# The second norm in groups of tiles, its scale row read from PSUM

## The chip, the cores and the metric

The kernel runs on one core of a Trainium2 chip. The metric is the device time of one execution in microseconds (us). A core has five engines with queues of their own, which run side by side and wait for one another through semaphores: TensorE (PE: matmuls), VectorE (DVE), ScalarE (ACT), GpSimd (POOL) and SyncE (SP, which here issues the plain DMAs). SBUF is the working memory with 128 partitions; PSUM holds the results of the matmuls and has 8 banks of 512 float32 numbers per partition. POOL works in SBUF here, never in PSUM.

## The reference

One decoder layer over 2048 tokens of 1024 channels: four mixers (RWKV-7, gated linear attention, mLSTM, latent attention), a projection, a first norm, and then a mixture of 32 experts of which each token takes two. The change is in what follows the experts:

```python
x = layer_norm(DN_ALPHA * x + mix, ln1_g[i], ln1_b[i], LN_EPS)
ffn = hier_moe(x, moe_w_rg[i], ...)
ple = jax.nn.sigmoid(x @ ple_w_gate[i] + ple_b_gate[i]) * (p[i] @ ple_w[i])
x = layer_norm(DN_ALPHA * x + ffn + ple, ln2_g[i], ln2_b[i], LN_EPS)
```

The last line is the second norm. For each token it takes the mean and the variance over 1024 channels, subtracts the mean, multiplies by the inverse root of the variance and by a scale row `g`, and adds a bias row `b`; the same two rows serve all tokens.

## The kernel before

The tokens are cut into 16 tiles of 128, with one token per partition and 1024 channels in the free dimension. Tiles lie in pairs 0 to 7. The experts add their results to `accd` in DRAM by indirect DMAs from POOL. When the last of these has landed, `finish` (L2202) reads `accd` pair by pair, normalizes and writes `out`. For the last four tiles (12 to 15, "late") the term `ple` is not yet in `accd`; `finish` and the end of the expert loop compute it: `late_gate` (48 matmuls into one of two PSUM tiles `self.gu` of two banks each, then two DVE additions of the gate's bias at L2187 and a tanh on ACT), `late_embed` (12 matmuls into the PSUM tile `yb`, then one DVE operation, L2200, that reads `yb`), and an addition to the tile on POOL (L2237).

`norm2(out, p)` treats one pair:

- a load of the pair into a raw tile (L2233); there are five of these, so pairs 5 and 7 wait for the outputs of pairs 0 and 1. Pair 4 goes into a tile of another pool, `m_dl`;
- the statistics of each tile: two `bn_stats` and one `bn_aggr` on DVE (L2253, L2254), or, for tiles 1, 3, 5, 7, 9 and 11 (`ACT_STATS`), four ACT passes (L2243) with three small DVE instructions among them (L2247 to L2249);
- the inverse root for both tiles at once, on DVE: L2256, then `rsqrt` (L68, L69 and three rounds of L71, L72, L73), then L2258. All of these handle two numbers per partition. Eight pairs make eight roots;
- the end of each tile. For most tiles ACT applies mean and root (L2265), DVE multiplies by `g` (L2266) and POOL adds `b` (L2267). For tiles 3, 7, 11, 14 and 15 (`DVE_ENDS`) DVE does all of it in two passes: L2262 with `g`, L2263 with `b`;
- the output of the tile by SP (L2268).

`g` and `b` lie in SBUF, in the tiles `m_xg` that held the gathered rows of the experts. The pairs come in the order 0, 1, 2, 3, 6, 4, 5, 7, with the late gates and embeddings written between them. Each queue runs in order, but the order isn't that of the text: a planner sorts the ready instructions of each queue by its own estimate of their times when the kernel is built, so that steps of a root lie between passes of other tiles.

Of the kernel before, what the change touches and what calls it, by code (L numbers as in the profile page):

```python
# [8 lines left out]
F32 = mybir.dt.float32  # L9
# [4 lines left out]
AF = mybir.ActivationFunctionType  # L14
OP = mybir.AluOpType
# [5 lines left out]
D = 1024  # L21
# [9 lines left out]
class Layer:  # L31
# [28 lines left out]
        nc.tensor.matmul(out, lh, rl, start=False, stop=False)  # L60
        nc.tensor.matmul(out, ll, rh, start=False, stop=stop)  # L61

    def rsqrt(self, v, y, n, tag):
        nc = self.nc
        t = self.sm.tile([128, n], F32, name="rs_t" + tag)
        ti = t.bitcast(I32)
        p = v.shape[0]
        nc.vector.tensor_scalar(ti[:p], v.bitcast(I32), 1, None, op0=OP.logical_shift_right)  # L68
        nc.vector.tensor_scalar(y.bitcast(I32), ti[:p], -1.0, float(0x5F3759DF), op0=OP.mult, op1=OP.add)  # L69
        for _ in range(3):  # L70
            nc.vector.tensor_mul(t[:p], y, y)  # L71
            nc.vector.scalar_tensor_tensor(t[:p], t[:p], -0.5, v, op0=OP.mult, op1=OP.mult)  # L72
            nc.vector.scalar_tensor_tensor(y, t[:p], 1.5, y, op0=OP.add, op1=OP.mult)  # L73
# [2101 lines left out]
    def late_gate(self, t):  # L2175
        nc = self.nc
        xh, xl, _ = self.lx.pop(t)
        banks = [self.gu[t % 2][:, j] for j in range(2)]
        for k in range(8):
            w = self.lg[k]  # L2180
            for i, (a, b) in enumerate(((xh, 0), (xh, 1), (xl, 0))):
                for j, p in enumerate(banks):
                    nc.tensor.matmul(p, a[:, k], w[:, b, j * 512:j * 512 + 512], start=k == 0 and i == 0, stop=k == 7 and i == 2)
        gt = self.mw.tile([128, D], F32, name="m_y", bufs=3)
        for j, p in enumerate(banks):
            g = slice(j * 512, j * 512 + 512)
            nc.vector.tensor_add(gt[:, g], p, self.ln2[2][:, g])  # L2187
        nc.scalar.activation(gt, gt, AF.Tanh, scale=0.5)
        self.lt[t] = gt
# [12 lines left out]
    def finish(self, out):  # L2202
        nc = self.nc
        t = T - self.LATE
        self.late_p(t)
        self.late_p(t + 1)
        self.late_x(t + 2)
        self.norm2(out, 0)
        self.late_turn(t + 2)
        self.late_gate(t + 1)  # L2210
        self.late_embed(t)
        self.late_p(t + 2)
        self.norm2(out, 1)
        self.late_turn(t + 3)
        self.norm2(out, 2)
        self.late_gate(t + 2)
        self.late_embed(t + 1)
        self.late_p(t + 3)
        self.late_gate(t + 3)
        self.norm2(out, 3)  # L2220
        self.late_embed(t + 2)
        self.late_embed(t + 3)
        self.norm2(out, t // 2)
        self.norm2(out, 4)
        self.norm2(out, 5)
        self.norm2(out, t // 2 + 1)

    def norm2(self, out, p):
        nc, G = self.nc, 2
        g, b, _ = self.ln2  # L2230
        mv = self.sm.tile([128, G, 2], F32, name="f_mv")
        z = self.raw_tile() if p != 4 else self.wdn.tile([128, 2, D], F32, name="m_dl")
        nc.sync.dma_start(out=z, in_=self.pairs(self.accd, p))  # L2233
        for i in range(G):
            t = p * G + i
            if t in self.lt:
                nc.gpsimd.tensor_add(z[:, i], z[:, i], self.lt.pop(t))  # L2237
            if t in self.ACT_STATS:
                a = self.sm.tile([128, 4], F32, name="f_a")
                for f in range(2):  # L2240
                    for j in range(2):
                        junk = self.mw.tile([128, 512], F32, name="m_t", bufs=3)
                        nc.scalar.activation(junk, z[:, i, j * 512:j * 512 + 512], (AF.Identity, AF.Square)[f], accum_out=a[:, 2 * f + j:2 * f + j + 1],  # L2243
                                             **({"bias": m} if f else {}))
                    if f == 0:
                        m = self.sm.tile([128, 1], F32, name="f_m")
                        nc.vector.tensor_scalar(m, a[:, 0:1], a[:, 1:2], -1.0 / D, op0=OP.add, op1=OP.mult)  # L2247
                nc.vector.tensor_scalar(mv[:, i, 0:1], m, -1.0, None, op0=OP.mult)
                nc.vector.tensor_scalar(mv[:, i, 1:2], a[:, 2:3], a[:, 3:4], 1.0 / D, op0=OP.add, op1=OP.mult)  # L2249
                continue  # L2250
            st = self.sm.tile([128, 2, 6], F32, name="ln_st")
            for j in range(2):
                nc.vector.bn_stats(st[:, j], z[:, i, j * 512:j * 512 + 512])  # L2253
            nc.vector.bn_aggr(mv[:, i], st.rearrange("p a b -> p (a b)"))  # L2254
        v, rs, sh = (self.sm.tile([128, G], F32, name="f_" + n) for n in ("v", "rs", "sh"))
        nc.vector.tensor_scalar(v, mv[:, :, 1], 1e-5, None, op0=OP.add)  # L2256
        self.rsqrt(v, rs, G, "f")
        nc.vector.scalar_tensor_tensor(sh, mv[:, :, 0], -1.0, rs, op0=OP.mult, op1=OP.mult)  # L2258
        for i in range(G):
            t, zi = p * G + i, z[:, i]  # L2260
            if t in self.DVE_ENDS:
                nc.vector.scalar_tensor_tensor(zi, zi, mv[:, i, 0:1], g, op0=OP.subtract, op1=OP.mult)  # L2262
                nc.vector.scalar_tensor_tensor(zi, zi, rs[:, i:i + 1], b, op0=OP.mult, op1=OP.add)  # L2263
            else:
                nc.scalar.activation(zi, zi, AF.Identity, scale=rs[:, i:i + 1], bias=sh[:, i:i + 1])  # L2265
                nc.vector.tensor_mul(zi, zi, g)  # L2266
                nc.gpsimd.tensor_add(zi, zi, b)  # L2267
            nc.sync.dma_start(out=out[t * 128:t * 128 + 128], in_=zi)  # L2268


def layer(ctx, tc, I, out):
# [115 lines left out]
```

## Time and profile before

| what | us |
|---|---|
| median of 3 runs | 3073.34 (3070.55 to 3081.36) |
| time of the profiled execution | 3073.2 |
| its span in the trace | 3071.4 |
| DVE busy | 1962.6 (64%) |
| ACT busy | 1224.2 (40%) |
| POOL busy | 888.6 (29%) |

The page gives the busy time of each engine and cuts the span into 40 slices. The timeline has one row for each instruction (or a run of equal ones, with their count): its start in us from the start of the span, its duration, engine, line, operation, and the tensors written and read; in brackets stands how long the engine had been idle and what it waited for. [...]

### The profile page before, as it was taken

The numbers are of one execution on the slowest core, as the hardware profiler recorded it, in microseconds if no ns is written. First come the engines' busy times: TensorE is split into PE (matmuls) and PEld (weight loads), VectorE is DVE, ScalarE is ACT, GpSimd is POOL, SyncE is SP. The second block draws the span as 40 slices with busy tenths as digits, with TensorE's granted clock in tenths as the row PEclk, the third lists the DMA queues.
The fourth block names the chain that finished last, engine by engine and source line by source line (L and its number), as shares of the span: only waits on it lengthen the run. The fifth ranks groups of instructions, "written<-read, shape, count | busy, mean of one in ns | idle before, by whom it ended". The sixth has DMA issues, their size and how long they took to land. (4 is left out here: it accounts for less than half of the span.)

```text
span 3071.4 us, 42829 instructions
## 1 busy us (share of the span) xinstructions
PE 2818.2 (92%) x15420; PEld 2219.4 (72%) x15421; DVE 1962.6 (64%) x4100; ACT 1224.2 (40%) x2001; POOL 888.6 (29%) x552
## 2 busy tenths in 40 slices
PE   8999999998989999999999999899889988999883
PEld 6898877777867766666477799777667767777662
DVE  6366364456555567766656645576687756687869
ACT  4222132222124433333310222165576756666852
POOL 1000000001010023424521201445464544645624
PEclk9999999989989898989999999999999989999996
DMA  6332242122225522200243412377587867877863
GB/s 189 102 99 71 68 127 69 54 73 58 52 57 162 173 58 78 62 26 18 95 146 131 138 62 69 136 251 258 174 294 259 264 213 223 284 244 261 303 229 137
DMA packets 287042, 442.98 MB, mean 144 GB/s; under 512 B 84088, under 2 KB 152040, under 8 KB 286760
## 3 DMA queue, kind: packets, MB, share of 16 engines
q1 hardware_dynamic: 272200, 397.78, 39.0%
q0 software_dynamic: 14560, 41.47, 5.5%
q8 instruction: 172, 2.82, 0.4%
q14 instruction: 110, 0.90, 0.1%
HBM read 350.52 MB, written 96.50 MB: 146 GB/s over the span
## 5 line engine op out<-in xcount | busy, mean ns | idle before, releaser
L1884 PE MATMUL m_g<-m_g,xhl 128*128 128x512 f32 x2032 | 520.9, 405 | 20.1 <-PEq L2011 10.1
L1884 PEld LDWEIGHTS m_g<-m_g,xhl 128*128 128x128 f32 x2032 | 376.2, 192 | 113.6 <-issue 33.7
L1836 DVE TENSOR_TENSOR m_g<-m_raw,m_g 128x1024 fp32r<-128x1024 f32 x188 | 267.0, 1448 | 90.9 <-ACT m_g L1835 88.7
L1835 ACT CAST m_g<-m_raw 128x1024 fp32r<-128x1024 f32 x252 | 255.3, 1057 | 96.5 <-PEq L2011 80.3
L1916 PE MATMUL m_y<-m_dh,m_h 128*128 128x512 f32 x656 | 226.0, 410 | 26.4 <-ACT m_y L1923 8.0
L59 PE MATMUL pbank<-xh,wh 128*128 128x512 f32 x544 | 226.8, 417 | 7.0 <-DVE us L213 3.6
L60 PE MATMUL pbank<-xl,wh 128*128 128x512 f32 x544 | 219.3, 403 | 0.0
L61 PE MATMUL pbank<-xh,wl 128*128 128x512 f32 x544 | 218.8, 403 | 0.0
L51 ACT CAST xhl<-bank 128x512 fp32r<-128x512 f32 x204 | 117.3, 607 | 245.2 <-PE bank L1408 243.9
L1836 POOL TENSOR_TENSOR m_g<-m_raw,m_g 128x1024 fp32r<-128x1024 f32 x64 | 185.0, 2966 | 91.1 <-ACT m_g L1835 53.6
L1466 PE MATMUL wide<-wt,xhl 128*128 128x512 f32 x768 | 182.8, 397 | 3.6 <-ACT xhl L51 3.6
L1836 POOL TENSOR_TENSOR m_dl<-m_raw,m_dh 128x1024 fp32r<-128x1024 f32 x64 | 179.4, 2845 | 14.8 <-ACT m_dh L1835 14.6
L1304 POOL TENSOR_TENSOR mla_acc<-mla_acc,mla_pt 128x512 f32<-128x512 f32 (+3 forms) x112 | 132.4, 1182 | 148.5 <-ACT mla_pt L1302 132.0
L1466 PEld LDWEIGHTS wide<-wt,xhl 128*128 128x128 f32 x768 | 143.6, 189 | 39.6 <-ACT xhl L51 7.4
L1916 PEld LDWEIGHTS m_y<-m_dh,m_h 128*128 128x128 f32 x656 | 129.1, 197 | 58.9 <-ACT m_y L1923 10.7
L1302 ACT ACTIVATE mla_pt<-sbank 128x512 f32<-128x512 f32 (+3 forms) x160 | 85.2, 533 | 213.0 <-PE sbank L1298 104.0
L52 DVE TENSOR_TENSOR xhl<-bank,xhl 128x512 fp32r<-128x512 f32 x204 | 136.4, 684 | 48.8 <-ACT xhl L51 46.7
L1930 POOL DMA_INDIRECT accd<-m_y,m_put x47 | 95.7, 2037 | 245.0 <-ACT m_y L1923 125.5
L1646 PE MATMUL gate<-wt,xhl 128*128 128x354 f32 (+1 forms) x864 | 149.6, 330 | 1.4 <-ACT xhl L51 1.0
L59 PE MATMUL pbank<-wh,xh 128*128 128x256 f32 x512 | 150.7, 294 | 0.0
L60 PE MATMUL pbank<-wl,xh 128*128 128x256 f32 x512 | 149.1, 291 | 0.0
L1916 PE MATMUL m_y<-m_dl,m_h 128*128 128x512 f32 x360 | 146.5, 407 | 2.2 <-POOL m_dl L1836 2.2
(642 smaller groups left out, 6309.8 us busy)
## 6 DMA issues: line engine op xcount, KB each, us to landing
m_raw<-in_moe_w_down SPq DMA_DIRECT2D x64, 1024.0 KB
m_raw<-in_moe_w_gate SPq DMA_DIRECT2D x126, 512.0 KB
m_raw<-in_moe_w_up SPq DMA_DIRECT2D x126, 512.0 KB
wraw<-in_w_in SPq DMA_DIRECT2D x80, 256.0 KB
o_x<-in_x SPq DMA_DIRECT2D x16, 512.0 KB
x1d<-m_g SPq DMA_DIRECT2D x16, 512.0 KB
accd<-wide SPq DMA_DIRECT2D x16, 512.0 KB
m_raw<-accd SPq DMA_DIRECT2D x7, 1024.0 KB
```

What stands on the lines that cost most here:

```text
L51: nc.scalar.copy(hi, src)
L52: (eng and nc.gpsimd or nc.vector).tensor_sub(lo, src, hi.bitcast(F32))
L59: nc.tensor.matmul(out, lh, rh, start=start, stop=False)
L60: nc.tensor.matmul(out, lh, rl, start=False, stop=False)
L61: nc.tensor.matmul(out, ll, rh, start=False, stop=stop)
L1304: (nc.vector if kt in self.SUMS else nc.gpsimd).tensor_add(acc[:, c0 * 128:512], acc[:, c0 * 128:512], pt[:, 0:n])
L1466: nc.tensor.matmul(p[:, j], a[:, k], W[k][bb][:, j * 512:j * 512 + 512], start=k == 0 and i == 0, stop=k == 7 and i == 2)
L1646: nc.tensor.matmul(p[:, 0:n], a[:, k], b[:, o:o + n], start=k == 0 and i == 0, stop=k == 7 and i == 2)
L1835: self.nc.scalar.copy(h[:, i], raw[:, i])
L1836: lo_eng.tensor_sub(l[:, i], raw[:, i], h[:, i].bitcast(F32))
L1884: self.mark["pe"] = self.nc.tensor.matmul(banks[:, j], a, b[:, k % 2, j * 512:j * 512 + 512], start=k == 0 and i == 0, stop=k == 7 and i = ...
L1916: self.nc.tensor.matmul(p[:, j], a, b[:, k % 2, j * 512:j * 512 + 512], start=k == 0 and i == 0, stop=k == 3 and i == len(ps) - 1)
```

## The change

The norm goes in groups of pairs: (0), (1, 2), (3, 4), (6, 5), (7). All tiles of a group share one root, so there are five roots, with two or four numbers per partition. The order of pairs becomes 0, 1, 2, 3, 4, 6, 5, 7. Of the two PSUM tiles in `self.gu`, the late gates now all use the first one; the second, which the experts are done with, receives a copy of the scale row `g` by two ACT copies at the start of `finish`, and L2262 and L2266 read `g` from there. The small tiles of the norm move to another pool. The diff, cut to its core:

```diff
@@ rsqrt
-        t = self.sm.tile([128, n], F32, name="rs_t" + tag)
+        t = pool.tile([128, 4], F32, name="rs_t" + tag)[:, 0:n] if pool else self.sm.tile([128, n], F32, name="rs_t" + tag)
@@ late_gate
-        banks = [self.gu[t % 2][:, j] for j in range(2)]
+        banks = [self.gu[0][:, j] for j in range(2)]
@@ finish
         self.late_x(t + 2)
+        self.gain = self.gu[1].rearrange("p j d -> p (j d)")
+        for j in range(2):
+            self.nc.scalar.copy(self.gu[1][:, j], self.ln2[0][:, j * 512:j * 512 + 512])
         self.norm2(out, 0)
         self.late_turn(t + 2)
         self.late_gate(t + 1)
         self.late_embed(t)
         self.late_p(t + 2)
-        self.norm2(out, 1)
         self.late_turn(t + 3)
-        self.norm2(out, 2)
+        self.norm2(out, 1, 2)
         self.late_gate(t + 2)
         self.late_embed(t + 1)
         self.late_p(t + 3)
         self.late_gate(t + 3)
-        self.norm2(out, 3)
+        self.norm2(out, 3, 4)
         self.late_embed(t + 2)
         self.late_embed(t + 3)
-        self.norm2(out, t // 2)
-        self.norm2(out, 4)
-        self.norm2(out, 5)
+        self.norm2(out, t // 2, 5)
         self.norm2(out, t // 2 + 1)
@@ norm2
-    def norm2(self, out, p):
-        nc, G = self.nc, 2
-        g, b, _ = self.ln2
-        mv = self.sm.tile([128, G, 2], F32, name="f_mv")
-        z = self.raw_tile() if p != 4 else self.wdn.tile([128, 2, D], F32, name="m_dl")
-        nc.sync.dma_start(out=z, in_=self.pairs(self.accd, p))
+    def norm2(self, out, *pp):
+        nc, n = self.nc, len(pp)
+        g, b = self.gain, self.ln2[1]
+        mv = self.mw.tile([128, 4, 2], F32, name="f_mv")[:, 0:2 * n]
+        Z = []
+        for p in pp:
+            z = self.raw_tile() if p != 4 else self.wdn.tile([128, 2, D], F32, name="m_dl")
+            nc.sync.dma_start(out=z, in_=self.pairs(self.accd, p))
+            Z += [(p * 2 + i, z[:, i]) for i in range(2)]
...
-        v, rs, sh = (self.sm.tile([128, G], F32, name="f_" + n) for n in ("v", "rs", "sh"))
+        v, rs, sh = (self.mw.tile([128, 4], F32, name="f_" + x)[:, 0:2 * n] for x in ("v", "rs", "sh"))
         nc.vector.tensor_scalar(v, mv[:, :, 1], 1e-5, None, op0=OP.add)
-        self.rsqrt(v, rs, G, "f")
+        self.rsqrt(v, rs, 2 * n, "f", self.mw)
```

## Rows read from the trace of the kernel before

**Rows 1.** The page, 40 equal slices of the span: VectorE's busy tenths.

```profile
DVE  6366364456555567766656645576687756687869
```

**Rows 2.** Stages: their length, each engine's busy time (count), granted clock, DMA share, GB/s.

```profile
core 0: us, PE busy (x) PEld busy (x) DVE busy (x) ACT busy (x) POOL busy (x), PEclk, DMA share, GB/s
...
2975.00:2981.00 6.00, 5.64 (x31) 4.77 (x32) 2.38 (x6) 1.95 (x5) 0.00 (x0) 1.00 0.76 271
...
2992.00:3004.00 12.00, 12.00 (x55) 9.88 (x54) 12.00 (x21) 4.61 (x11) 8.00 (x3) 1.00 0.27 109
...
3050.00:3060.00 10.00, 0.00 (x0) 0.00 (x0) 10.00 (x16) 2.11 (x3) 5.55 (x2) 0.50 0.25 105
```

**Rows 3.** Groups by line, 2980.7 to 3067.5, DVE and POOL: busy, mean, idle before.

```profile
L72 DVE SCALAR_TENSOR_TENSOR rs_tf<-rs_tf,f_v 128x2 f32<-128x2 f32 x24 | 15.1, 634 | 0.1
...
L71 DVE TENSOR_TENSOR rs_tf<-f_rs 128x2 f32<-128x2 f32 x24 | 10.8, 452 | 0.0
L2266 DVE TENSOR_TENSOR m_raw<-m_raw,m_xg 128x1024 f32<-128x1024 f32 x9 | 10.7, 1215 | 0.0
L73 DVE SCALAR_TENSOR_TENSOR f_rs<-rs_tf,f_rs 128x2 f32<-128x2 f32 x24 | 10.5, 442 | 0.1
...
L2200 DVE SCALAR_TENSOR_TENSOR m_y<-m_y 128x1024 f32<-128x1024 f32 x4 | 4.8, 1209 | 0.0
...
L2267 POOL TENSOR_TENSOR m_raw<-m_raw,m_xg 128x1024 f32<-128x1024 f32 x9 | 23.8, 2651 | 17.8 <-DVE m_raw L2266 13.2 <-DVE rs_tf L71 4.5
L2237 POOL TENSOR_TENSOR m_raw<-m_raw,m_y 128x1024 f32<-128x1024 f32 x4 | 11.3, 2833 | 35.1 <-ACT m_t L2243 26.0 <-DVE m_y L2200 9.1
```

**Rows 4.** Timeline of DVE: small instructions between other work, and alone at the end.

```profile
3003.17 0.16 DVE L2256 TENSOR_SCALAR f_v<-f_mv 128x2 f32<-128x2 f32 x1
3003.24 0.68 DVE L2187 TENSOR_TENSOR m_y<-m_g,m_xg 128x512 f32<-128x512 f32 x1
...
3064.43 0.16 DVE L72 SCALAR_TENSOR_TENSOR rs_tf<-rs_tf,f_v 128x2 f32<-128x2 f32 x1
3064.63 0.16 DVE L73 SCALAR_TENSOR_TENSOR f_rs<-rs_tf,f_rs 128x2 f32<-128x2 f32 x1
```

**Rows 5.** Timeline from 3020, DVE and POOL: start, duration, instruction.

```profile
3020.88 5.58 POOL L2267 TENSOR_TENSOR m_raw<-m_raw,m_xg 128x1024 f32<-128x1024 f32 x2 [7.05 <-DVE m_raw L2266]
...
3021.85 1.28 DVE L2187 TENSOR_TENSOR m_y<-m_g,m_xg 128x512 f32<-128x512 f32 x2
...
3024.09 1.21 DVE L2200 SCALAR_TENSOR_TENSOR m_y<-m_y 128x1024 f32<-128x1024 f32 x1
3025.22 1.26 DVE L73 SCALAR_TENSOR_TENSOR f_rs<-rs_tf,f_rs 128x2 f32<-128x2 f32 x1
```

**Rows 6.** Timeline: an add that ran alone, and L2262 beside two adds.

```profile
3026.43 2.36 POOL L2237 TENSOR_TENSOR m_raw<-m_raw,m_y 128x1024 f32<-128x1024 f32 x1
...
3051.55 5.55 POOL L2267 TENSOR_TENSOR m_dl<-m_dl,m_xg 128x1024 f32<-128x1024 f32 x2 [4.12 <-DVE m_dl L2266]
...
3054.82 3.37 DVE L2262 SCALAR_TENSOR_TENSOR m_raw<-m_raw,f_mv,m_xg 128x1024 f32<-128x1024 f32 x1
```

**Rows 7.** The stretch from 2992.1 for L71, L72 and L73 alone: busy time (count).

```profile
2992.10:3067.40 75.30, 10.24 (x21) 0.69 0.34 134
...
2992.10:3067.40 75.30, 14.68 (x21) 0.69 0.34 134
...
2992.10:3067.40 75.30, 10.08 (x21) 0.69 0.34 134
```

**Rows 8.** Timeline: first add, last gate, pair 7's load, ACT's longest wait, last root.

```profile
2992.47 2.40 POOL L2237 TENSOR_TENSOR m_raw<-m_raw,m_y 128x1024 f32<-128x1024 f32 x1 [26.02 <-ACT m_t L2243]
...
2998.76 11.15 PE L2183 MATMUL m_g<-m_g,xhl 128*128 128x512 f32 x48
...
3016.53 0.38 SPq L2233 DMA_DIRECT2D m_raw<-accd  x1
...
3017.20 0.72 ACT L2243 ACTIVATE m_t<-m_dl,f_m 128x512 f32<-128x512 f32 x1 [8.16 <-DVE f_m L2247]
...
3054.75 0.16 DVE L2256 TENSOR_SCALAR f_v<-f_mv 128x2 f32<-128x2 f32 x1
```

More of the change, by code (lines that the diff above doesn't have):

```diff
@@ L61, in mm3, with rsqrt @@
         nc.tensor.matmul(out, ll, rh, start=False, stop=stop)
-    def rsqrt(self, v, y, n, tag):
+    def rsqrt(self, v, y, n, tag, pool=None):
         nc = self.nc
-        t = self.sm.tile([128, n], F32, name="rs_t" + tag)
+        t = pool.tile([128, 4], F32, name="rs_t" + tag)[:, 0:n] if pool else self.sm.tile([128, n], F32, name="rs_t" + tag)
         ti = t.bitcast(I32)
@@ L2219, in finish @@
         self.late_gate(t + 3)
-        self.norm2(out, 3)
+        self.norm2(out, 3, 4)
         self.late_embed(t + 2)
         self.late_embed(t + 3)
-        self.norm2(out, t // 2)
-        self.norm2(out, 4)
-        self.norm2(out, 5)
+        self.norm2(out, t // 2, 5)
         self.norm2(out, t // 2 + 1)
-    def norm2(self, out, p):
-        nc, G = self.nc, 2
-        g, b, _ = self.ln2
-        mv = self.sm.tile([128, G, 2], F32, name="f_mv")
-        z = self.raw_tile() if p != 4 else self.wdn.tile([128, 2, D], F32, name="m_dl")
-        nc.sync.dma_start(out=z, in_=self.pairs(self.accd, p))
-        for i in range(G):
-            t = p * G + i
+    def norm2(self, out, *pp):
[7 more added lines that the diff above has]
+            Z += [(p * 2 + i, z[:, i]) for i in range(2)]
+        for i, (t, z) in enumerate(Z):
             if t in self.lt:
-                nc.gpsimd.tensor_add(z[:, i], z[:, i], self.lt.pop(t))
+                nc.gpsimd.tensor_add(z, z, self.lt.pop(t))
             if t in self.ACT_STATS:
@@ L2242, in norm2 @@
                         junk = self.mw.tile([128, 512], F32, name="m_t", bufs=3)
-                        nc.scalar.activation(junk, z[:, i, j * 512:j * 512 + 512], (AF.Identity, AF.Square)[f], accum_out=a[:, 2 * f + j:2 * f + j + 1],
+                        nc.scalar.activation(junk, z[:, j * 512:j * 512 + 512], (AF.Identity, AF.Square)[f], accum_out=a[:, 2 * f + j:2 * f + j + 1],
                                              **({"bias": m} if f else {}))
@@ L2252, in norm2 @@
             for j in range(2):
-                nc.vector.bn_stats(st[:, j], z[:, i, j * 512:j * 512 + 512])
+                nc.vector.bn_stats(st[:, j], z[:, j * 512:j * 512 + 512])
             nc.vector.bn_aggr(mv[:, i], st.rearrange("p a b -> p (a b)"))
-        v, rs, sh = (self.sm.tile([128, G], F32, name="f_" + n) for n in ("v", "rs", "sh"))
+        v, rs, sh = (self.mw.tile([128, 4], F32, name="f_" + x)[:, 0:2 * n] for x in ("v", "rs", "sh"))
         nc.vector.tensor_scalar(v, mv[:, :, 1], 1e-5, None, op0=OP.add)
-        self.rsqrt(v, rs, G, "f")
+        self.rsqrt(v, rs, 2 * n, "f", self.mw)
         nc.vector.scalar_tensor_tensor(sh, mv[:, :, 0], -1.0, rs, op0=OP.mult, op1=OP.mult)
-        for i in range(G):
-            t, zi = p * G + i, z[:, i]
+        for i, (t, z) in enumerate(Z):
             if t in self.DVE_ENDS:
-                nc.vector.scalar_tensor_tensor(zi, zi, mv[:, i, 0:1], g, op0=OP.subtract, op1=OP.mult)
-                nc.vector.scalar_tensor_tensor(zi, zi, rs[:, i:i + 1], b, op0=OP.mult, op1=OP.add)
-            else:
[L2265 to L2268, printed above, removed]
+                nc.vector.scalar_tensor_tensor(z, z, mv[:, i, 0:1], g, op0=OP.subtract, op1=OP.mult)
+                nc.vector.scalar_tensor_tensor(z, z, rs[:, i:i + 1], b, op0=OP.mult, op1=OP.add)
+            else:
+                nc.scalar.activation(z, z, AF.Identity, scale=rs[:, i:i + 1], bias=sh[:, i:i + 1])
+                nc.vector.tensor_mul(z, z, g)
+                nc.gpsimd.tensor_add(z, z, b)
+            nc.sync.dma_start(out=out[t * 128:t * 128 + 128], in_=z)
 def layer(ctx, tc, I, out):
```

## The prediction

> **What bounds the kernel now.** I read the page first. In its 40 slices VectorE (DVE) rises to the end and stands at 9 in the last one [rows 1], and the diff touches nothing ahead of the last 95 us. So the question belongs to that tail, and I cut it into stages. From 2992 on DVE is busy for every microsecond of each stage until 3060; TensorE has nothing to do at the end, ScalarE (ACT) stands at a third or less and GpSimd (POOL) at a half to two thirds [rows 2]. A queue that is always busy sets the end, so I asked what DVE does in those 75 us. The groups by line show it: the steps of the root (L71 to L73), which handle two numbers per partition, cost as much as the passes over whole tiles, with means of 442 to 634 ns [rows 3], where an undisturbed step takes 0.16 us (the last two of the tail) [rows 4].
>
> In order of time the reason is plain. A root step that begins while POOL runs one of its adds (L2237, L2267) ends when that add ends: the step of 3025.22 ends at 3026.48, the add pair of 3020.88 ends at 3026.46. Between those two stalls a DVE pass of full size, L2200, ran beside the second add in its usual 1.21 us, and the two L2187 ran beside the first one in 1.28 us together [rows 5]. The difference is in the operands: L2187 and L2200 take one operand from PSUM, the root steps take both from SBUF. L2262, with the scale row in SBUF, took 3.37 us beside the adds of 3051.55, 2.1 more than passes of its size take (1.2 to 1.3); and two adds of which the first began beside the second of two L2266 took 5.58 us, 0.9 more than twice the 2.36 of one alone [rows 5, 6]. So a DVE instruction with two SBUF operands and a POOL add exclude each other, whole instruction by whole instruction.
>
> How much is that? After 2992.1 there are 3 x 21 = 63 root steps, busy for 10.24 + 14.68 + 10.08 = 35.0 us [rows 7]. At 0.155 each they would take 9.8, so 25.2 us are lost in them, in 14 long steps of 1.1 to 2.4 us; L2262 adds 2.1 [rows 6]. Together 27.3 us in 15 stalls, 1.8 each, and POOL makes exactly 15 adds in the tail, L2237 for the four late tiles and L2267 for the eleven whose end is not on DVE alone (nine of them on raw tiles, two on pair 4's) [rows 3]: each one stops DVE once.
>
> **The change part by part.** *Three roots fewer.* A root is 13 small instructions (L2256, L68, L69, nine steps, L2258). Laid between other work, one costs 0.07 us to the start of the next; alone, 0.20 [rows 4]. Three roots are 2.7 us by the first price and 7.8 by the second; against that, the remaining roots lose neighbours and may move from the first price towards the second, so the lower end is 0. I take 3.0, near the first price, because most steps in the rows lie between other work.
>
> *The scale row in PSUM.* Eleven L2266 and five L2262 now have one SBUF operand. Their own time stays: L2200, with a PSUM operand of the same 1024 elements, has a mean of 1209 ns, L2266 1215 [rows 3]. [...] What the move brings is that L2262 no longer waits (2.1 us) and that L2266 no longer holds an add back: where now the second L2266 of a pair delays the first add by 0.9 and root steps then wait for both adds, the first add will start at the end of the first L2266 and run beside those that follow. L2263 still reads its row from SBUF.
>
> *Copies to PSUM.* Two ACT copies of 128x512 (an ACT pass of that size takes 0.72 us [rows 8]) fall in a stage in which ACT is busy for 1.95 of 6 us [rows 2]: nothing. Without that cover they would put 1.4 us ahead of the first statistics.
>
> *One pair of gate banks.* Every late gate now waits for the previous one's L2187. The last gate's matmuls began at 2998.76; they took 11.15 us; the L2187 ahead of them ended at 3003.9, so they would begin some 5 us later and end at about 3015. Their own L2187 ran only at 3021.85 [rows 4, 5, 8]: nothing, up to 5 us if DVE should reach that point by 3010.
>
> *Grouping.* A root now waits for the statistics of four tiles, and their outputs and buffers come later. The load of pair 7 waits for pair 1's two outputs; it was issued at 3016.53, and its tiles' root began at 3054.75, 38 us later [rows 8]. Two adds of 2.4 and four passes of statistics have to lie between, so most of the 38 us is to spare, also with the output writes that SyncE's queue holds ahead of it. Nothing. ACT's statistics are the other side: a tile needs two passes with a DVE instruction (L2247) between, and ACT has waited 8.16 us for that [rows 8]. While DVE has other work this is free; exposed, it is a tile's four halves of 0.72, 2.9 us, for the five such tiles in groups of four: 0 to 14 us. I take 0, since DVE was never idle in the stretch.
>
> *Which stalls remain.* Of the 15 adds I count six as covered: the one at 2992.47 on tile 12 [rows 8], which stopped a step of the second root, a root that will not have begun; the first add in each of the groups (0), (1,2), (3,4), (6,5), beside which one or two further L2266 of 1.13 us run; and one near the end, beside the L2262 of tiles 14 and 15. Nine are left. Each meets a root step as before, since one DVE step slips in between two adds and the next one waits. With more tiles' passes to lie between steps I take 1.7 each, 15.3 us. The ends are two stalls (3.6) and all fifteen (27.3).
>
> **The sum.** In the profiled execution DVE ended at 3067.4, the span at 3071.4 (the last output's 4.0 us, which remain), the time is 3073.2, 1.8 more; the median of the runs is 3073.34, the same. DVE's end without any stall and with three roots fewer: 3067.4 - 27.3 - 3.0 = 3037.1. With the nine stalls 3052.4, and with 4.0 and 1.8: **3058 us**, 15 below now.
>
> **The rivals.** *More is covered.* Statistics, gates and embeddings of the late tiles are mostly one-operand or PSUM passes; if the order lays them beside the adds, two to five stalls remain: 3042.9 + 3.6 to 9 = 3047 to 3052. For it: L2200 between two stalls. Against: near the end few such passes are left, and L2262, a stall then, came right behind another one [rows 6].
>
> *The adds find a step all the same.* Three adds in a row, a queue in order, and roots that are ready early: every add costs its 1.8 again, or DVE idles that long at the fourfold root. 3042.9 + 27.3 = 3070. The same comes out if an operand in PSUM does not free L2266; the rows on L2187 and L2200 say that it does, so this is a small part of the case.
>
> *Slower: the groups go serial.* A root step costs 0.07 us where something lies beside it [rows 4]. If a group's root has nothing beside it, every add stops DVE for its full 2.36 us (35.4 for 15) and ACT's 14 us of statistics lie open: 3042.9 + 49 = 3092. It decides from stalls and idle time of 40 us together, which gives 3083. Against it: ACT has two thirds of the tail free [rows 2], and statistics can be done far ahead of their root.
>
> **How the numbers follow.** Forecast 0.56 (3053 to 3064); more covered 0.16; about the same 0.22; slower 0.06. About 0.3%, 9.2 us, is what a measurement of this kernel can tell from no change, so faster means under 3064.1 and slower over 3082.6: 0.72, 0.22, 0.06. The range goes from two stalls (3046) to all fifteen (3070); what is left out is the slower case and idle time on top of fifteen stalls.
>
> **What would show it.** Five L2256 in place of eight. L2262 and L2266 at 1.2 to 1.3 us each, the longest too. The adds of POOL: still 15, all near 2.36. Root steps over 1 us: about nine. DVE's last instruction near 3052 and no idle time before it. I am wrong in the step on stalls if the long steps are still 14; in the step on grouping if DVE waits for ACT or for a load; in the step on PSUM if an L2266 still ends together with an add; and in the step on the gate bank if TensorE's late matmuls end last.

## The result, and the profile after

The changed kernel takes 3056.31 us (median of 20 runs, 3044.25 to 3081.61), the kernel before 3077.73 in the same series (20 runs, one of them of 4306.74 us, which moves this median by 0.2): a ratio of 0.9932 (95% interval 0.9916 to 0.9948). A second series of 12 runs gave 0.9962 (0.9942 to 0.9982), while the kernel before against itself gave 0.9994 (0.9979 to 1.001). The change makes the kernel faster, by some 0.4 to 0.7%.

Single executions scatter by 30 to 40 us; where a kernel was traced twice, the scatter lay ahead of the part that was changed. The traces measure that part far better: from the issue of the first load of `accd` to the end of the span the kernel before takes 3071.4 - 2975.40 = 96.0 us, and 96.1 in a second trace; the changed kernel takes 3063.8 - 2980.43 = 83.4, and 83.4 in a second trace. I call this stretch the **tail**; all comparisons below are of tails. The change takes 12.6 us off it.

The lines of the changed kernel are numbered a little higher: L2257 are the statistics (before: L2253), L2260 the start of the root (L2256), L2265 and L2266 the two DVE passes of an end (L2262, L2263), L2269 the product with `g` (L2266), L2270 and L2241 POOL's additions (L2267, L2237). The groups by line over the tail, as in [rows 3]: busy us, mean ns, idle time before them:

```profile
L2269 DVE TENSOR_TENSOR m_raw<-m_raw,m_g 128x1024 f32<-128x1024 f32 x9 | 10.8, 1216 | 1.5 <-ACT m_raw L2268 1.2 <-issue 0.2
L2266 DVE SCALAR_TENSOR_TENSOR m_raw<-m_raw,f_rs,m_xg 128x1024 f32<-128x1024 f32 x5 | 7.9, 1600 | 0.0
L2265 DVE SCALAR_TENSOR_TENSOR m_raw<-m_raw,f_mv,m_g 128x1024 f32<-128x1024 f32 x5 | 6.3, 1270 | 0.0
...
L72 DVE SCALAR_TENSOR_TENSOR rs_tf<-rs_tf,f_v 128x4 f32<-128x4 f32 (+1 forms) x15 | 4.5, 303 | 0.4
...
L71 DVE TENSOR_TENSOR rs_tf<-f_rs 128x4 f32<-128x4 f32 (+1 forms) x15 | 3.6, 239 | 0.4
...
L73 DVE SCALAR_TENSOR_TENSOR f_rs<-rs_tf,f_rs 128x4 f32<-128x4 f32 (+1 forms) x15 | 2.4, 160 | 0.4
...
L2270 POOL TENSOR_TENSOR m_raw<-m_raw,m_xg 128x1024 f32<-128x1024 f32 x9 | 23.2, 2595 | 45.4 <-DVE m_raw L2269 31.5 <-issue 7.8 <-DMA m_raw<-accd 6.1
L2241 POOL TENSOR_TENSOR m_raw<-m_raw,m_y 128x1024 f32<-128x1024 f32 x4 | 9.5, 2372 | 0.0
```

The 45 root steps take 10.5 us together where 72 took 36.4 [rows 3]. POOL makes the same 15 additions. No pass that reads `g` waits for an addition any more (a mean of 1216 ns for L2269, as before, and 1270 for L2265, where L2262 had one of 3.37 us [rows 6]). The long instructions that remain, in order of time, with one of 0.84 us at L2260 ahead of them:

```profile
3022.30 1.29 DVE L2257 BATCH_NORM_STATS2 ln_st<-m_raw 128x6 f32<-128x512 f32 x2 [2.82 <-POOL m_raw L2241]
...
3025.56 0.16 DVE L72 SCALAR_TENSOR_TENSOR rs_tf<-rs_tf,f_v 128x4 f32<-128x4 f32 x1
3025.76 0.16 DVE L73 SCALAR_TENSOR_TENSOR f_rs<-rs_tf,f_rs 128x4 f32<-128x4 f32 x1
...
3037.03 1.33 DVE L71 TENSOR_TENSOR rs_tf<-f_rs 128x4 f32<-128x4 f32 x1
3038.39 2.29 DVE L72 SCALAR_TENSOR_TENSOR rs_tf<-rs_tf,f_v 128x4 f32<-128x4 f32 x1
...
3049.00 2.74 DVE L2266 SCALAR_TENSOR_TENSOR m_raw<-m_raw,f_rs,m_xg 128x1024 f32<-128x1024 f32 x1
```

Two root steps over 1 us where there were 14, and one L2266, which reads the bias row from SBUF. But there is something new: in the first row DVE was idle for 2.82 us, waiting for POOL. The stages (columns as in [rows 2]) show how much DVE idles:

```profile
2987.60:2998.00 10.40, 10.40 (x47) 8.62 (x46) 9.08 (x33) 7.95 (x20) 0.00 (x0) 1.00 0.99 379
...
3010.00:3024.00 14.00, 9.59 (x32) 7.47 (x31) 10.58 (x17) 8.12 (x17) 10.37 (x4) 0.76 0.53 194
...
3030.00:3041.00 11.00, 8.30 (x31) 6.38 (x30) 10.90 (x13) 1.96 (x2) 10.41 (x4) 0.84 0.48 191
```

Of 14 us from 3010 on DVE is busy for 10.58; before, it was busy throughout [rows 2]. And the tail begins later. These rows are TensorE's first matmuls of tile 13's gate, SyncE's first load and DVE's first statistics:

```profile
2980.44 2.47 PE L2183 MATMUL m_g<-m_g,xhl 128*128 128x512 f32 x5 [12.37 <-DVEq L2099]
...
2980.43 1.57 SPq L2237 DMA_DIRECT2D m_raw<-accd  x3
...
2987.64 1.28 DVE L2257 BATCH_NORM_STATS2 ln_st<-m_raw 128x6 f32<-128x512 f32 x2
```

TensorE sat idle for 12.37 us ahead of that gate, until the branch of L2099 was through, and the first statistics began 7.2 us after the load's issue, not 5.4 as before (2980.81 - 2975.40).

### The profile page after: what moved, and what is told of

Read it like the earlier page. It is cut to its first block, busy times and chain, and to the rows that moved or that the text cites. A ratio compares the mean times of both kernels' runs of the same rounds, so it can differ in the third digit from the quotient of the medians.

```text
span 3063.8 us, 42798 instructions
## 1 busy us (share of the span) xinstructions
PE 2826.6 (92%) x15420; PEld 2225.7 (73%) x15421; DVE 1934.6 (63%) x4061; ACT 1225.6 (40%) x2003; POOL 887.9 (29%) x552
## 3 DMA queue, kind: packets, MB, share of 16 engines
q8 instruction: 172, 2.82, 0.4%
## 5 line engine op out<-in xcount | busy, mean ns | idle before, releaser
L1884 PE MATMUL m_g<-m_g,xhl 128*128 128x512 f32 x2032 | 521.0, 404 | 16.4 <-PEq L2011 9.1
L1836 DVE TENSOR_TENSOR m_g<-m_raw,m_g 128x1024 fp32r<-128x1024 f32 x188 | 273.5, 1482 | 109.7 <-ACT m_g L1835 104.4
L1916 PEld LDWEIGHTS m_y<-m_dh,m_h 128*128 128x128 f32 x656 | 128.6, 196 | 57.1 <-issue 10.8
L1930 POOL DMA_INDIRECT accd<-m_y,m_put x47 | 96.1, 2044 | 247.2 <-ACT m_y L1923 148.1
L61 PE MATMUL pbank<-wh,xl 128*128 128x256 f32 x512 | 149.1, 291 | 0.0
```

Source lines behind the costliest of these rows:

```text
L1836: lo_eng.tensor_sub(l[:, i], raw[:, i], h[:, i].bitcast(F32))
L1884: self.mark["pe"] = self.nc.tensor.matmul(banks[:, j], a, b[:, k % 2, j * 512:j * 512 + 512], start=k == 0 and i == 0, stop=k == 7 and i = ...
L1916: self.nc.tensor.matmul(p[:, j], a, b[:, k % 2, j * 512:j * 512 + 512], start=k == 0 and i == 0, stop=k == 3 and i == len(ps) - 1)
```

## The experiments

The theory that the prediction rests on (A): DVE and POOL exclude each other when a DVE instruction has two operands in SBUF; each of the 15 additions stops DVE once; the change keeps additions and such instructions apart, through fewer roots and through the row in PSUM. The rivals: (B) the number of roots decides, not where the row lies; (C) the root steps are slow in themselves or by their semaphores. The whole table first; "stalls" is what DVE's instructions of the tail took beyond their usual time, each long instruction taken from the timeline less 0.16 us for a root step and 1.24 for a pass of 1024; "idle" is DVE's after the first statistics.

| kernel | tail | load to first statistics | stalls | idle | ratio of times (95%) |
|---|---|---|---|---|---|
| before | 96.0 | 5.4 | 27.8 | 0.5 | 1 |
| before, again | 96.1 | 5.4 | 27.9 | 0.5 | 0.9994 (0.9979 to 1.001) |
| groups alone | 94.3 | 5.2 | 28.7 | 0.5 | 0.9975 (0.9953 to 0.9997) |
| PSUM row alone | 90.5 | 7.2 | 15.2 | 2.6 | 0.9978 (0.995 to 1.0006) |
| one gate tile alone | 100.2 | 6.3 | 27.6 | 1.7 | 1.0004 (0.9987 to 1.0021) |
| the change | 83.4 | 7.2 | 5.8 | 6.9 | 0.9932 (0.9916 to 0.9948) |
| the change, again | 83.4 | 7.2 | 5.8 | 6.9 | 0.9962 (0.9942 to 0.9982) |
| the change, PSUM tiles swapped | 81.4 | 5.0 | 11.7 | 3.5 | 0.9945 (0.9918 to 0.9972) |
| PSUM row alone, tiles swapped | 89.0 | 5.2 | 19.1 | 1.2 | one run |
| before without the bias additions | 75.8 | 5.7 | 7.2 | 0.4 | 0.9921 (0.9896 to 0.9947) |
| the change without them | 80.2 | 7.2 | 4.2 | 5.0 | 0.9918 (0.989 to 0.9946) |
| swapped, last embedding in the gates' tile | 79.5 | 5.2 | 11.7 | 1.3 | 0.9931 (0.9905 to 0.9956) |
| the same, tile 10's statistics on ACT | 83.6 | 4.7 | 14.4 | 4.5 | one run |

What is left of a tail without start, stalls and idle time and without the last output (4.0 to 4.3 us) is DVE's **own work**: 96.0 - 5.4 - 27.8 - 0.5 - 4.0 = 58.3 us before. The planner gives DVE's queue another order with nearly every edit, so a row measures an edit together with its order. The two runs without the bias additions keep most of theirs: 178 of the 187 DVE instructions behind the first statistics stand, by their lines, in the order of the kernel before, and 136 of 149 in that of the change.

**Groups alone.** The changed kernel with the row left in SBUF and the gates on alternating tiles:

```diff
-        self.gain = self.gu[1].rearrange("p j d -> p (j d)")
-        for j in range(2):
-            self.nc.scalar.copy(self.gu[1][:, j], self.ln2[0][:, j * 512:j * 512 + 512])
+        self.gain = self.ln2[0]
...
-        banks = [self.gu[0][:, j] for j in range(2)]
+        banks = [self.gu[t % 2][:, j] for j in range(2)]
```

> Grouping alone: five roots, the scale row still in SBUF, the late gates on alternating banks. Theory A (the scale row in PSUM frees the passes that run beside the adds of POOL, and grouping alone moves the meeting from root steps to the passes with g): L2266 and L2262 end together with adds, some 8 to 12 stalls of 1 to 2.3 us in all, so 3060 to 3072 where the kernel before has 3077, that is a ratio of 0.994 to 0.998. Theory B (fewer, denser roots alone keep the adds away from two-operand work): about the ratio of the whole change, 0.992 to 0.994, and under 6 us of stalls.

The tail is 94.3 us, 1.7 under that of before, with 28.7 us of stalls: as much as before, in 14 rows of the timeline, where 8 to 12 were expected. B is out: five roots without the row in PSUM gain next to nothing. The stalls have moved. These rows (L2267 is the product with `g` here, L2268 POOL's addition) show it; DVE first, then POOL:

```profile
3001.62 2.33 DVE L69 TENSOR_SCALAR f_rs<-rs_tf 128x4 int32<-128x4 int32 x1
...
3013.52 5.61 DVE L2267 TENSOR_TENSOR m_raw<-m_raw,m_xg 128x1024 f32<-128x1024 f32 x3
...
3001.51 2.42 POOL L2239 TENSOR_TENSOR m_raw<-m_raw,m_y 128x1024 f32<-128x1024 f32 x1
...
3014.78 6.54 POOL L2268 TENSOR_TENSOR m_raw<-m_raw,m_xg 128x1024 f32<-128x1024 f32 x2 [6.37 <-DVE m_raw L2267]
```

Three products take 5.61 us where three of 1.13 to the start of the next (from 3012.93 to 3014.06 in the changed kernel) would take 3.5, and two additions take 6.54 where 4.7 would do: they go by turns. In the changed kernel POOL makes three additions in a row from 3011.90 on, and the two products that begin beside them run through:

```profile
3011.90 8.03 POOL L2270 TENSOR_TENSOR m_raw<-m_raw,m_xg 128x1024 f32<-128x1024 f32 x3 [6.12 <-DMA m_raw<-accd]
...
3012.93 1.22 DVE L2269 TENSOR_TENSOR m_raw<-m_raw,m_g 128x1024 f32<-128x1024 f32 x1
...
3015.30 1.21 DVE L2269 TENSOR_TENSOR m_raw<-m_raw,m_g 128x1024 f32<-128x1024 f32 x1
```

**The PSUM row alone**, with eight roots and the pairs in the old order; the late gates stay on one PSUM tile, as in the change:

```diff
-        self.norm2(out, 1, 2)
+        self.norm2(out, 1)
+        self.norm2(out, 2)
...
-        self.norm2(out, 3, 4)
+        self.norm2(out, 3)
...
-        self.norm2(out, t // 2, 5)
+        self.norm2(out, t // 2)
+        self.norm2(out, 4)
+        self.norm2(out, 5)
```

> The scale row in PSUM and one pair of gate banks, with eight roots of two tiles in the old order of pairs. Theory A: L2262 and L2266 never wait, but each add still meets a root step, 10 to 13 long steps near 2 us; ratio 0.995 to 1.000. Theory B: no gain, ratio 0.998 to 1.002, since the number of roots decides. If the PSUM row alone gave the whole gain, ratio 0.992 to 0.994 with under 5 long steps.

Stalls fall to 15.2 us, in seven instructions over 1 us and one pass with the bias row, fewer than A expected; the tail to 90.5. So the row in PSUM, with its one gate tile, does about half of it by itself, and the two parts together more than the sum (28.7 and 15.2 against 27.8, both 5.8). I read this so that a root with no addition beside it needs both the products that run through and fewer roots to place; no run shows that by itself. Two rows of DVE and one of POOL carry a further point, to which the last section comes back:

```profile
3033.06 0.09 DVE L2255 TENSOR_SCALAR f_mv<-f_m 128x1 f32<-128x1 f32 x1
3033.07 2.27 DVE L68 TENSOR_SCALAR rs_tf<-f_v 128x2 int32<-128x2 int32 x1
...
3032.95 2.37 POOL L2244 TENSOR_TENSOR m_raw<-m_raw,m_y 128x1024 f32<-128x1024 f32 x1
```

**One gate tile alone**, in the kernel before:

```diff
-        banks = [self.gu[t % 2][:, j] for j in range(2)]
+        banks = [self.gu[0][:, j] for j in range(2)]
```

> The kernel before with nothing changed but the late gates on one PSUM tile. As read from the trace of the changed kernel: the gate of tile 13 now waits for the branch of the general case, which writes the same PSUM tile, so TensorE is idle for some 12 us ahead of it and the first statistics begin 1 to 2 us later behind the turned tile. Expected 1 to 5 us slower than before, ratio 1.0003 to 1.002. Rival, that this is hidden: ratio 0.999 to 1.001 and the statistics start as early after the last load as before.

The tail is 4.2 us longer than before; in the times this is within their interval. TensorE shows the same idle time as in the changed kernel:

```profile
2980.20 2.47 PE L2183 MATMUL m_g<-m_g,xhl 128*128 128x512 f32 x5 [12.56 <-DVEq L2099]
```

The reason is in the code. `moe_general`, the branch for experts with many tokens, stands ahead of `finish` at L2099 and writes `self.gu[0]`; it isn't taken, but what uses that tile has to stay behind it. The gate of tile 13 used `self.gu[1]` and ran ahead of the branch (from 2965.16 on in the kernel before); on `self.gu[0]` it can't. TensorE then turns tile 14 later, and the first statistics stand in DVE's and ACT's queues behind that tile's splits (here DVE's split of 2985.92, 0.69 us, and the statistics right behind it at 2986.53). This start is 0.9 of the 4.2 us; 1.2 are idle time and 2.2 are DVE's own work (60.5 against 58.3), which comes in another order.

**The PSUM tiles swapped** in the changed kernel, so that only tile 12's gate uses the first one:

```diff
-        banks = [self.gu[0][:, j] for j in range(2)]
+        banks = [self.gu[t != T - self.LATE][:, j] for j in range(2)]
...
-        self.gain = self.gu[1].rearrange("p j d -> p (j d)")
+        self.gain = self.gu[0].rearrange("p j d -> p (j d)")
         for j in range(2):
-            self.nc.scalar.copy(self.gu[1][:, j], self.ln2[0][:, j * 512:j * 512 + 512])
+            self.nc.scalar.copy(self.gu[0][:, j], self.ln2[0][:, j * 512:j * 512 + 512])
```

> The changed kernel with the two PSUM tiles swapped: the gate of tile 12 stays in the first, those of tiles 13 to 15 go to the second, and the scale row is copied to the first. If the gate of tile 13 behind the branch costs time, it starts ahead of the branch again as in the kernel before, and the time is 2 to 5 us under that of the changed kernel: ratio to before 0.9905 to 0.9925. If it is hidden behind other work: 0.993 as the change.

The statistics begin 5.0 us after the load, 2.2 earlier than in the change, and the tail is 2.0 us under that of the change, at the lower edge of what was expected; the ratio of 0.9945 lies above the expected 0.9905 to 0.9925, and the times don't separate the two. Behind the start the sum hardly changes, but its parts trade places: idle time and stalls are 3.5 and 11.7 us here, 6.9 and 5.8 in the change, and DVE's own work is 57.1 against 59.5. It fits the rows, but no run shows it by itself, that with the gates in time DVE reaches its roots sooner and meets additions there, while with the gates late it idles and the additions pass meanwhile. Of the idle time 2.27 us lie in one place, behind TensorE's last embedding (12 matmuls, 5.45 us, 0.43 to 0.50 from one to the next where those of the embedding ahead of it have 0.23; TensorE had been idle for 2.63 us before them):

```profile
3037.39 1.22 DVE L2200 SCALAR_TENSOR_TENSOR m_y<-m_y 128x1024 f32<-128x1024 f32 x1 [2.27 <-PE m_y L2197]
```

The swapped tiles with eight roots complete the comparison:

> The scale row in PSUM with eight roots, as in the run of the PSUM row alone (90.5 us from the load of the first pair to the end), with the PSUM tiles swapped so that the gate of tile 13 doesn't wait for the branch. If the bank cost 4 us there as in the kernel before (100.2 against 96.0), the stretch is 86 to 87 us, and grouping on top of it (81.4) is worth 5. If the order of the queue eats what the bank gives, it is 89 to 91.

The tail is 89.0 us, 1.5 under that of the row alone on unswapped tiles, not 4: here, too, stalls rise with the earlier start (19.1 against 15.2 us). Grouping on top of it is worth 89.0 - 81.4 = 7.6 us, though grouping by itself gave 1.7.

**Without the bias additions**, in the kernel before and in the changed one; in eleven tiles the bias is missing from the output:

```diff
-                nc.gpsimd.tensor_add(zi, zi, b)
```

> The kernel before with the eleven POOL additions of the bias row (L2267) left out, so the bias is missing in eleven tiles. If the adds of POOL are what stops DVE (theory A), only the four L2237 remain and stall it: from the load of the first pair to the end 96 us become 74 to 80, and at most 5 long root steps remain. If the root steps are slow for another reason (a rival: their chains, the semaphores between them), the stretch shrinks by no more than the last add's wait, to 92 to 95.

> The changed kernel with the same eleven additions left out. Theory A: little of its 83.4 us is due to adds (5.8 us of stalls in all), so the stretch becomes 77 to 82, near that of the kernel before without its adds: the change then is worth under 4 us instead of 12.6. If the change gained by fewer roots or otherwise, the distance to the kernel before stays at 10 us or more without the adds as well.

The kernel before loses 20.2 us of its 96.0, with nothing taken from DVE. The same groups as in [rows 3], in the kernel before without the additions:

```profile
L72 DVE SCALAR_TENSOR_TENSOR rs_tf<-rs_tf,f_v 128x2 f32<-128x2 f32 x24 | 7.6, 316 | 0.1
...
L71 DVE TENSOR_TENSOR rs_tf<-f_rs 128x2 f32<-128x2 f32 x24 | 5.2, 218 | 0.0
...
L73 DVE SCALAR_TENSOR_TENSOR f_rs<-rs_tf,f_rs 128x2 f32<-128x2 f32 x24 | 3.6, 150 | 0.1
...
L2237 POOL TENSOR_TENSOR m_raw<-m_raw,m_y 128x1024 f32<-128x1024 f32 x4 | 10.5, 2634 | 51.7 <-DMA m_dl<-accd 27.5 <-DVE rs_tf L71 12.5 <-DVE f_sh L2258 6.7
```

The same 72 steps take 16.4 us, not 36.4. C is out. The changed kernel loses only 3.2 us by the same cut, and without the additions its tail is 80.2 - 75.8 = 4.4 us *longer* than that of the kernel before. So all of the gain, and 4.4 us more, is in how DVE and these additions meet; for the rest the change costs.

**The series repeated.**

> The changed kernel once more, for its ratio and a second trace. The trace of the profiled execution shows 12.6 us less from the load of the first pair on, the timed runs 16 to 26. If the tail explains all, the stretch is 82 to 85 again and the ratio comes out at 0.995 to 0.996; if the rest lies ahead of the tail, the ratio stays at 0.993 with the same stretch.

> The kernel before as it is, against itself, for the spread of the measurement and of its tail: ratio 0.998 to 1.002; if the stretch from the load of the first pair on is fixed by the order of the queues it is 95 to 97 us again, if the stalls depend on chance it differs by several us.

Both tails come out within 0.1 us of the first traces, with DVE's instructions in the same order. The change repeats stall by stall; in the kernel before one of the 15 stalls falls on a product with `g` in place of the first long root step. So it is the order of the queues that sets the tail, with hardly any chance. 12.6 us are 0.41%, which is within the interval of the second series, but not within that of the first (0.52 to 0.84%). Nor is the rest seen ahead of the tail: from the clearing of `m_g` at L1849, with which the experts begin, to the first load of `accd` the kernel before takes 999.4 and 998.2 us in its two traces (2975.4 - 1976.0, 2985.0 - 1986.8), the change 1000.3 and 1000.9 (2980.4 - 1980.1, 2974.3 - 1973.4). Over all traces that stage varies from 991 to 1003 us, so these do not size a difference of a few us there. Why the first series came out further off is open.

**A version that is faster in the trace.** The swapped kernel, with the last embedding's matmuls in the gates' tile, which is free by then, so that they don't wait for the L2200 ahead of them:

```diff
         eh, el = self.le
+        yb = self.gu[1] if t == T - 1 else self.yb
...
-                    self.nc.tensor.matmul(self.yb[:, j], ...)
+                    self.nc.tensor.matmul(yb[:, j], ...)
...
-        ... self.yb.rearrange("p a b -> p (a b)"), op0=OP.add, op1=OP.mult)
+        ... yb.rearrange("p a b -> p (a b)"), op0=OP.add, op1=OP.mult)
```

> The changed kernel with the PSUM tiles swapped (81.4 us from the load of the first pair to the end), and the last embedding's matmuls into the gates' PSUM tile in place of the one that the embedding before it still fills. In the swapped kernel DVE was idle for 2.3 us at L2200, which waited for those matmuls, and these for the previous L2200. If that wait decides, the stretch is 78 to 80; if DVE only meets the adds of POOL sooner instead, it stays at 81 to 82.

> The same with the statistics of tile 10 on ACT in place of DVE, which takes 1.3 us from DVE and gives ACT 2.9. If DVE's queue still sets the end, the stretch is some 1 us under that of the run without it; if the group's root waits for ACT, it is up to 3 us longer.

The tail is 79.5 us, 3.9 under that of the change and 16.5 under before; the ratio of 0.9931 lies beside both of the change's, so the times alone don't say that it is better. The embedding's matmuls now run right behind the one before, and L2200 (L2201 here) no longer waits. In the trace of the change the matmuls of the embedding before the last follow one another 0.23 us apart, at a granted clock of 1.00 (3031.67 to 3034.50), and those of the last one 0.38 to 0.43 apart, at 0.54 (3037.25 to 3040.50). Two things changed here at once: the 12 matmuls begin 2.4 us earlier after the first load, and they take 3.0 us in place of 5.45, with 0.23 to 0.27 from one to the next:

```profile
3030.35 0.70 PE L2198 MATMUL m_g<-m_dh,m_h 128*128 128x512 f32 x2
...
3034.57 1.21 DVE L2201 SCALAR_TENSOR_TENSOR m_y<-m_y,m_g 128x1024 f32<-128x1024 f32 x1
```

With tile 10's statistics on ACT the tail is 83.6, longer by 4.1, more than either expectation allowed, though DVE has less to do: idle time and stalls rise by 3.2 and 2.7 us. DVE's work alone is not the measure of this tail; who meets whom counts as much.

## Why the prediction was right, and where its steps were not

The forecast of 3058 us, with 15 us gained, is within 2 us of the first median, and 2.4 us more than the gain that the tails show. That the time agrees so well is partly luck: the forecast started from a median of 3073.34, the series gave 3077.73, and the gain between the medians was 21.4 us in the first series and 14.6 in the second, of which the tails show 12.6. The mechanism stands: the runs without the additions show that they stopped DVE, and the run of the groups alone that the row in PSUM is what lets the products run through. But the sum was right by terms that were off in both directions. Against before, in the tail:

| term | forecast | measured |
|---|---|---|
| stalls | -12.0 (27.3 to 15.3) | -22.0 (27.8 to 5.8) |
| DVE idle | 0 | +6.4 |
| first statistics later | 0 | +1.8 |
| DVE's own work, with three roots fewer | -3.0 | +1.2 |
| last output | 0 | 0 |
| sum | -15.0 | -12.6 |

- *Which stalls remain.* This term was mis-sized: nine stalls of 1.7 us were forecast, and there are 5.8 us in all, nearly all of it in four instructions: 11 of the 15 additions hold nothing up for long, where six were counted as covered. Part of the reason is that the roots of the groups (1, 2), (3, 4) fell into times in which POOL had nothing to add, and DVE ran their steps in a row (the rows at 3025). The swapped kernel, which has its gates in time, has 11.7 us.
- *The scale row in PSUM*: right. L2269 and L2265 never wait for an addition. Their own time stays: a mean of 1216 ns for the product with `g` from PSUM (L2269), where it was 1215 from SBUF (L2266 [rows 3]).
- *Three roots fewer*: near right as a saving, but not what became of DVE's own work. By the table of the runs grouping takes 2.4 us off it with the row in SBUF (58.3 to 55.9), 2.0 with the row in PSUM (61.5 to 59.5) and 2.3 on swapped tiles (59.4 to 57.1), where 3.0 was forecast. What the sum lacked is that the other parts of the change raise it: with eight roots, 2.2 by the one gate tile alone (60.5) and 3.2 by the row in PSUM with it (61.5); with the gates in time the row's part is 1.1 (59.4). Together it rose by 1.2. Up to 0.6 of that is a split of tile 14 that has slid behind the first statistics. The rest fits root steps that have lost their company: in the change 41 of the 65 small instructions of the roots have the next one of a root right behind them, 0.18 to 0.22 us later (3025.56 to 3025.76); before it were 5 of 104, and in the groups alone 6 of 65. So it is not the grouping as such that moved them to the dearer price; I take it to be the new order of the queue, but no run shows that alone.
- *Copies to PSUM*: nothing, as forecast; on swapped tiles, which have the copies too, the statistics begin 5.0 us after the load, against 5.4 before.
- *One pair of gate banks*: wrong. The step named the L2187 ahead of a gate as what it waits for, and had looked only at the last gate. The prediction took it that nothing ahead of the last 95 us is touched, but in the kernel before the gate of tile 13 began at 2965.16, ten us ahead of the first load. In the change it waits for the branch that writes the same tile, which a reading of `moe_general` would have shown. It costs 1.8 us at the start, and 4.2 in the kernel before.
- *Grouping*: the load of pair 7 was issued at 3022.3 and was indeed not late. But DVE was not busy throughout: it waited 2.82 us for POOL's addition to tile 13, as the late gates and the order of the queue had pushed the embedding of tile 13 behind the ends of group (1, 2). I took 0 of 0 to 14; it was 6.4, with the gates' share in it.
- *The rivals.* Of *More is covered* the stalls came true (3.6 to 9 us, measured 5.8), but not the time of 3047 to 3052, as idle time, the later start and DVE's own work together took back 9.4 us. That the groups go serial did occur, as idle time of 6.4 us and as roots alone, but far under the 40 us from which it would have decided. That the additions find a step all the same is what the groups alone did, with 28.7 us. The case against the serial rival rested on ACT at a third or less; in the stage from 3017 to 3030 it was busy for 7.03 of 13 us.

## What to carry to other kernels

When a tiny instruction has a mean of several hundred ns, look at what the neighbouring engine does when it ends: here 15 stalls of DVE were 15 additions of POOL, and a row that many passes share was worth moving to PSUM only so that these passes no longer wait for the additions (one of them 3.37 us [rows 6], and none over 1.3 in the change). A queue that is full and stalled doesn't give back what you take from it one for one: three roots fewer saved 2.0 to 2.4 us in each comparison, but small steps that lost the work beside them took it back, and an earlier start came with more stalls. When a buffer gets a second use, look for every writer of it, also for those in a branch that never runs: here TensorE sat idle for 12.37 us behind one.

## What the runs showed of the hardware

I had not expected that small one-operand instructions wait as well. L68 and L69 (shift and subtraction on two or four numbers, one operand from SBUF) and the root's first addition (L2260) end with POOL's addition: 2.33 us for L69 beside the addition of 3001.51 in the run of the groups alone, 2.27 for L68 in that of the PSUM row, and 0.84 for the L2260 of 3004.97 in the change, beside the addition of 3003.38 (2.40 us). A TENSOR_SCALAR on a single number per partition did not: 0.09 us at 3033.06, beside the same addition that then held L68. The statistics, also with one operand, are not held up in any trace (0.63 to 0.70 us throughout). So the prediction's rule, two operands in SBUF, was too narrow; what sets the waiting one-operand instructions apart from the others, no run shows.

Over all thirteen traces there is no exception. I counted the DVE instructions that began inside one of POOL's additions, with at least 0.3 us of it to go. Of those with two tensors in SBUF, all 53 small ones ended 0.01 to 0.03 us after the addition and all 18 passes 1.08 or 1.09 us after it; all 37 TENSOR_SCALAR on two or four numbers ended 0.02 or 0.03 us after it. The 84 with an operand in PSUM, the 30 statistics, their 24 aggregations and the 40 TENSOR_SCALAR on one number took what they take elsewhere: in the changed kernel 0.67 to 0.68 us for an L2187 and 1.20 to 1.22 for an L2200 or L2269 beside an addition, 0.64 to 0.70 for a statistics instruction, 0.19 to 0.20 for an aggregation, 0.14 to 0.21 for a TENSOR_SCALAR on one number.

Between two additions in a row one waiting DVE instruction slips in, and the next one waits for the whole of the following addition: in the kernel before, the step L71 of 2997.89 ended at 3000.23 with the addition of 2996.96, and the L72 of 3000.28 took 2.30 us, to the end of the addition of 3000.17. So, too, in the groups alone, where three products (5.61 us) and two additions (6.54) took turns.
